# A decoder layer in split float32: Strassen's seven products for gate and up, plain products for down, the embedding projection first, SBUF placed by hand

## The chip, the cores and the metric

One core of a Trainium2 chip runs the whole program. The metric is the device time of one execution in microseconds (us); the kernel before takes 2062.82 us (median of 3 runs, 2061.0 to 2064.16). The engines are TensorE (PE, matrix products; its weight loads are PEld), VectorE (DVE), ScalarE (ACT), GpSimd (POOL) and SyncE (SP, which here only issues transfers).

## The reference

One layer over 1056 tokens (1024 of a prompt, 8 samples of 4), width 1024:

```
x = x + 1/2 * SwiGLU_1(RMSNorm(x))        # gate, up: 1024 -> 2816; down: 2816 -> 1024
z = RMSNorm(x) @ w_in                     # q, k, v | gate B | gate C | h
x = x + concat([window_attention(q, k, v), B * dwconv3(C * h)]) @ w_out
x = x + 1/2 * SwiGLU_2(RMSNorm(x))
x = x + sigmoid(RMSNorm(x) @ w_ple_gate) * (p @ w_ple_proj)      # p: 1056 x 256
```

It also returns the last keys, values and convolution inputs. All is float32; SwiGLU is (silu(h Wg) * (h Wu)) Wd.

## The kernel before

Activations lie transposed: 128 of the features in the partitions, 8 such tiles, the tokens along the row. The tokens are cut into three chunks `c` of 384, 384 and 288. Every float32 operand is kept as a high part in the fast format float32r and a low part with what is left over, and each product of two tiles takes three matmuls into one PSUM bank: high by high, high by low, low by high (`mm_group`, L264 to L270; in the convolution part `proj2`, L790 to L792). A product over 1024 inputs is thus a group of 24 matmuls.

Weights come in units of 128 x 1024 from DRAM by SP into two raw buffers, in the order in which they are used; ACT copies the high part (L110), DVE subtracts for the low part (L111), up to five units ahead. `tick` after each group splits a unit and runs deferred pieces.

The program runs: FFN 1; the input projection with attention and convolution; the output projection; FFN 2; the gated embedding. An FFN (`ffn`, L282) goes through its 22 blocks of 128 hidden features in six batches; for each block the gate and up groups of the three chunks, then DVE (L305, L307, L308), ACT (L306 tanh, L311) and POOL (L309) make the hidden tile h as a high and a low part in SBUF, then the batch's share of down is added into x by DVE (L325). The norm's factor is applied to what comes out of the products, so the products wait only for x times a gain (`prep`, L235, L236).

Attention is a list of 9 pieces of work (the samples, then 8 query blocks), which are dealt out between the halves of the convolution's groups: scores (L627, L630), scores with bias on DVE (L637), softmax on DVE, ACT and POOL (L644 to L657), transposes (L665), the product with the values (L674). One buffer each for the scores and their transposes serves all blocks. A chunk's part of the result (`mix`) is split for the output projection when its blocks are done (`split_mix`, L805, L806), and x is then read back from DRAM into a buffer of its own per chunk (L811). The output projection's groups (L878 on) add into x (L881); the first two chunks' come ahead of the third's.

The embedding projection (6 matmuls a group, L937 on) is done at the end, between the groups of the last gate. The order of each engine's instructions is set by the framework's scheduler, which simulates the program and takes from the emitted order what is ready; an engine then runs its list strictly in that order.

## Time and profile before

| | |
|---|---|
| runs | 2061.0 to 2064.16 us, median 2062.82 |
| profiled execution: span from first to last instruction | 2060.6 us (the median of the runs is 2.2 us above it; no other time of this execution is given) |
| PE busy | 2050.2 us, 12683 matmuls recorded |
| DVE, ACT, POOL busy | 960.3, 501.5, 287.2 us |
| share of PE in the chain that ended last | 97% |
| transferred | 118.06 MB, mean 57 GB/s |

The busy time of PE is the union of its matmuls' durations. These overlap: a matmul starts while the one before it still drains. What a matmul costs is therefore read from the distance between starts in the timeline and not from its mean duration. The chain of waits follows the last instruction back to what released it; its shares tell which engine's work would have to shrink.

### The profile page before, as it was taken

To read this page: it belongs to the slowest core of one execution; us is meant where nothing else is said; L and a number is where in the kernel's file an instruction comes from. 1 tells how busy PE (TensorE), PEld (TensorE's weight loads), DVE (VectorE), ACT (ScalarE), POOL (GpSimd) and SP (SyncE) were. 2 spreads that over 40 slices of the span, in tenths; PEclk is the share of its full clock that TensorE was granted. 3 is DMA by queue.
4 is the path that set the end of the run, shared out by engine and by line. 5 is a ranking of instruction groups with operands and counts; after the bars stand their busy time and mean duration, and the time that the engine had idled before them with its cause. 6 is when DMAs were issued, how large, how long until landed. Compare 5 with 4: busy or idle time off the path is not lost.

```text
span 2060.6 us, 29941 instructions
## 1 busy us (share of the span) xinstructions
PE 2050.2 (99%) x12683; PEld 2007.9 (97%) x12683; DVE 960.3 (47%) x1809; ACT 501.5 (24%) x917; POOL 287.2 (14%) x335
## 2 busy tenths in 40 slices
PE   9999999999999999999999999999999999999999
PEld 9999999999999999988888999999999999999999
DVE  6343433433334366466773764343333343344843
ACT  6121120211211243233442421212112022023410
POOL 3201010110100142022221220101101001012300
PEclk9999999999999999999999999999999999999999
DMA  7211110211111124111131211111111021111121
GB/s 263 76 54 42 52 52 11 83 41 51 43 32 62 42 102 136 35 31 32 31 93 36 70 52 41 49 38 50 40 52 52 21 72 42 31 62 52 59 71 39
DMA packets 37673, 118.06 MB, mean 57 GB/s; under 512 B 7697, under 2 KB 12185, under 8 KB 36644
## 3 DMA queue, kind: packets, MB, share of 16 engines
q1 hardware_dynamic: 35780, 112.05, 16.9%
q0 software_dynamic: 1472, 4.00, 0.7%
q8 instruction: 99, 1.62, 0.3%
q14 instruction: 34, 0.28, 0.0%
q10 hardware_dynamic: 288, 0.10, 0.0%
HBM read 106.26 MB, written 11.58 MB: 57 GB/s over the span
## 4 chain that ended last, share of the span: by engine, by line
PE 97%; DVE 2%; DMA 1%; ACT 0%; issue 0%; POOL 0%; ACTq 0%; DVEq 0%; POOLq 0%
PE ps L269 29%; PE ps L268 29%; PE ps L270 28%; PE ps L790 2%; PE ps L791 2%; PE ps L792 2%; PE ps L630 1%; PE ps L674 1%; PE ps L627 1%; PE ps L665 1%; PE ps L570 0%; DVE xnl L236 0%; DVE xr L325 0%; DVE wlo L111 0%; DVE nt L209 0%; DMA wraw<-in_wpg_dram 0%
## 5 line engine op out<-in xcount | busy, mean ns | idle before, releaser
L268 PE MATMUL ps<-xnh,whi 128*128 128x384 f32 (+1 forms) x2448 | 786.8, 322 | 1.2 <-ACT whi L110 1.2
L269 PE MATMUL ps<-xnh,wlo 128*128 128x384 f32 (+1 forms) x2448 | 786.7, 322 | 0.8 <-DVE wlo L111 0.8
L270 PE MATMUL ps<-xnl,whi 128*128 128x384 f32 (+1 forms) x2448 | 786.2, 321 | 0.0
L269 PEld LDWEIGHTS ps<-xnh,wlo 128*128 128x128 f32 x2448 | 460.0, 188 | 1.3 <-DVE wlo L111 1.1
L268 PEld LDWEIGHTS ps<-xnh,whi 128*128 128x128 f32 x2448 | 459.8, 188 | 1.5 <-ACT whi L110 1.4
L270 PEld LDWEIGHTS ps<-xnl,whi 128*128 128x128 f32 x2448 | 460.1, 188 | 0.2
L269 PE MATMUL ps<-hh,wlo 128*128 128x384 f32 (+1 forms) x1056 | 343.8, 326 | 0.0
L268 PE MATMUL ps<-hh,whi 128*128 128x384 f32 (+1 forms) x1056 | 341.5, 324 | 0.0
L270 PE MATMUL ps<-hl,whi 128*128 128x384 f32 (+1 forms) x1056 | 336.7, 320 | 0.0
L110 ACT CAST whi<-wraw 128x1024 fp32r<-128x1024 f32 x166 | 173.1, 1051 | 615.9 <-PE ps L270 523.0
L309 POOL TENSOR_TENSOR a<-a,rb 128x384 f32<-128x384 f32 x132 | 128.9, 977 | 1235.8 <-DVE a L308 1230.3
L111 DVE TENSOR_TENSOR wlo<-wraw,whi 128x1024 fp32r<-128x1024 f32 x166 | 213.5, 1290 | 106.8 <-ACT whi L110 106.6
L270 PEld LDWEIGHTS ps<-hl,whi 128*128 128x128 f32 x1056 | 198.1, 188 | 0.9 <-DVE hl L312 0.6
L269 PEld LDWEIGHTS ps<-hh,wlo 128*128 128x128 f32 x1056 | 198.1, 188 | 0.5
L268 PEld LDWEIGHTS ps<-hh,whi 128*128 128x128 f32 x1056 | 197.6, 187 | 0.3
L311 ACT CAST hh<-a 128x384 fp32r<-128x384 f32 x132 | 64.3, 487 | 366.9 <-POOL a L309 366.9
L305 DVE TENSOR_TENSOR a<-ps,rb 128x384 f32<-128x384 f32 x132 | 69.1, 524 | 178.3 <-PE ps L270 174.7
L312 DVE TENSOR_TENSOR hl<-a,hh 128x384 fp32r<-128x384 f32 x132 | 68.8, 521 | 152.0 <-ACT hh L311 152.0
L325 DVE SCALAR_TENSOR_TENSOR xr<-ps,xr 128x384 f32<-128x384 f32 (+1 forms) x144 | 75.2, 523 | 132.8 <-PE ps L270 132.6
L325 DVE SCALAR_TENSOR_TENSOR x<-ps,x 128x384 f32<-128x384 f32 (+1 forms) x144 | 75.1, 522 | 133.0 <-PE ps L270 132.9
L308 DVE TENSOR_TENSOR a<-a,ps 128x384 f32<-128x384 f32 x132 | 68.8, 521 | 126.3 <-PE ps L270 125.7
L306 ACT ACTIVATE th<-a 128x384 f32<-128x384 f32 x132 | 65.5, 496 | 225.8 <-DVE a L305 225.7
(190 smaller groups left out, 1828.6 us busy)
## 6 DMA issues: line engine op xcount, KB each, us to landing
wraw<-in_w1gu_dram SPq DMA_DIRECT2D x44, 512.0 KB
wraw<-in_w2gu_dram SPq DMA_DIRECT2D x44, 512.0 KB
wraw<-in_w1d_dram SPq DMA_DIRECT2D x22, 512.0 KB
wraw<-in_w2d_dram SPq DMA_DIRECT2D x22, 512.0 KB
wraw<-in_win_dram SPq DMA_DIRECT2D x18, 512.0 KB
xtok<-in_xtok_dram SPq DMA_DIRECT2D x8, 512.0 KB
wraw<-in_wout_dram SPq DMA_DIRECT2D x8, 512.0 KB
wraw<-in_wpg_dram SPq DMA_DIRECT2D x8, 512.0 KB
```

The source lines that it names most:

```text
L110: nc.scalar.copy(out=hi, in_=raw)
L111: nc.vector.tensor_tensor(out=lo, in0=raw, in1=hi.bitcast(F32), op=ALU.subtract)
L268: nc.tensor.matmul(ps[:, :W], lhsT=wh, rhs=xh, start=(k == 0), stop=False)
L269: nc.tensor.matmul(ps[:, :W], lhsT=wl, rhs=xh, start=False, stop=False)
L270: nc.tensor.matmul(ps[:, :W], lhsT=wh, rhs=xl, start=False, stop=(k == n - 1))
L305: nc.vector.tensor_tensor(out=a[:, :W], in0=psg[:, :W], in1=rb, op=ALU.mult)
L306: nc.scalar.activation(out=th[:, :W], in_=a[:, :W], func=AF.Tanh, scale=0.5)
L308: nc.vector.tensor_tensor(out=a[:, :W], in0=a[:, :W], in1=ps[:, :W], op=ALU.mult)
L309: nc.gpsimd.tensor_tensor(out=a[:, :W], in0=a[:, :W], in1=rb, op=ALU.mult)
L311: nc.scalar.copy(out=hh[j][:, sl], in_=a[:, :W])
L312: nc.vector.tensor_tensor(out=hl[j][:, sl], in0=a[:, :W], in1=hh[j][:, sl].bitcast(F32), op=ALU.subtract)
L325: nc.vector.scalar_tensor_tensor(out=x[c][:, m], in0=ps[:, :W], scalar=0.25, in1=x[c][:, m], op0=ALU.mult, op1=ALU.add)
```

## The change

**Gate and up.** The first three blocks of hidden features are still computed plainly (`lead_group`), now as 2 x 2 quarters: two output rows (gate, up), two halves of the inputs, two halves of a token chunk. Tokens are cut into two chunks of 528 here, with halves of 264. For the other 19 blocks Strassen's scheme (in Winograd's form) replaces the 8 quarter products by 7 (`Quad`, `segment`): each is 4 tiles x 3 matmuls of 264 columns. The four weight sums are made by POOL per block, the four sums of activations once per chunk; all are split into high and low parts as before. A segment interleaves products 1, 5, 2, 6 of one chunk with 7, 3, 4 of the one before.

**Down.** h goes to DRAM (`hd`) and comes back in chunks of 384, 384 and 288; down runs over two halves of 11 hidden tiles, in groups of 33 matmuls (`DownProj`).

**Norms of the FFNs.** Their factor is now multiplied into x in place before the products (`n_stat`, `n_y`); x is read again from DRAM for down.

**Embedding projection.** It runs first, as 32 half groups of 6 matmuls, and its result waits in DRAM (`pp_d`).

**Memory.** `at` places nearly everything by hand in one arena. In the output projection x is one region again, over the place of `mix`; its units 22 to 25 (rows m = 4 to 7) have their weights where the keys, the values and the bias lay (`WOUT2`). The order is chunk by chunk.

The core of the diff:

```diff
+    def unit_at(i):
+        return WOUT2[i - 22] if 22 <= i < 26 else UAT[(i - 26 if i > 25 else i) % 4]
     def can_split():
-        return st["split"] < len(units) and st["split"] < st["done"] + HL
+        i = st["split"]
+        room = st["done"] >= 18 if 22 <= i < 26 else i < st["done"] + HL
+        return i < st["end"] and room
...
+    OPS = (1, 5, 2, 6, 7, 3, 4)
+    class Weights:
+        def __init__(self, gu, j):
+            r = wload(gu, j)
+            s = [at("ws", WS + 512 * i, 512) for i in range(4)]
+            add = nc.gpsimd.tensor_tensor
+            add(out=s[0], in0=r[2], in1=r[3], op=ALU.add)
+            add(out=s[1], in0=s[0], in1=r[0], op=ALU.add)
+            add(out=s[2], in0=r[0], in1=r[2], op=ALU.add)
+            add(out=s[3], in0=s[1], in1=r[1], op=ALU.add)
+            self.of = {1: r[0], 2: r[1], 3: s[3], 4: r[3], 5: s[0], 6: s[1], 7: s[2]}
+            self.w = {}
+        def split(self, o):
+            self.w[o] = whl(WAT[o])
+            split(self.w[o][0], self.w[o][1], self.of[o])
+        def __getitem__(self, o):
+            return self.w[o]
...
+    class Quad:
+        def __init__(self, w, c):
+            self.w, self.ch, self.follow = w, c, None
+        def product(self, o, ps, start):
+            wh, wl = self.w[o]
+            for k in range(4):
+                ks = slice(k * P, (k + 1) * P)
+                last = k == 3
+                bh, bl = op_k(self.ch, o, 0, k), op_k(self.ch, o, 1, k)
+                nc.tensor.matmul(ps[:, :HH], lhsT=wh[:, ks], rhs=bh, start=(start and k == 0), stop=False, skip_group_check=True)
+                nc.tensor.matmul(ps[:, :HH], lhsT=wl[:, ks], rhs=bh, start=False, stop=False, skip_group_check=True)
+                nc.tensor.matmul(ps[:, :HH], lhsT=wh[:, ks], rhs=bl, start=False, stop=last, skip_group_check=True)
+        def step(self, o):
+            if o == 1:
+                self.b = psb()
+            elif o == 5:
+                self.c = psb()
+            elif o == 2:
+                self.a = psb()
+            ps = self.b if o in (1, 6, 7, 4) else self.c if o in (5, 3) else self.a
+            self.product(o, ps, o in (1, 5, 2))
+            getattr(self, f"out{o}")()
+            if self.follow:
+                self.follow.split(o)
+    def segment(q, p):
+        for o, of in ((1, q), (5, q), (7, p), (2, q), (6, q), (3, p), (4, p)):
+            if of:
+                of.step(o)
...
+    class GateUp(Quad):
+        def __init__(self, w, j, c):
+            super().__init__(w, c)
+            self.j = j
+            self.g = g_tile()
+        def silu(self, i):
+            th = th_tile()
+            g = self.g[:, i]
+            nc.scalar.activation(out=th, in_=g, func=AF.Tanh, scale=0.5)
+            nc.vector.scalar_tensor_tensor(out=g, in0=th, scalar=1.0, in1=g, op0=ALU.add, op1=ALU.mult)
+        def out1(self):
+            nc.scalar.copy(out=self.g[:, 0], in_=self.b[:, :HH])
+        def out5(self):
+            pass
+        def out2(self):
+            nc.vector.tensor_tensor(out=self.g[:, 0], in0=self.a[:, :HH], in1=self.g[:, 0], op=ALU.add)
+            self.silu(0)
+        def out6(self):
+            nc.scalar.copy(out=self.g[:, 1], in_=self.b[:, :HH])
+        def out7(self):
+            self.u = wtile("u", shape=[P, HH])
+            nc.vector.tensor_copy(out=self.u, in_=self.c[:, :HH])
+            nc.vector.scalar_tensor_tensor(out=self.u, in0=self.b[:, :HH], scalar=-1.0, in1=self.u, op0=ALU.mult, op1=ALU.subtract)
+        def out3(self):
+            nc.vector.tensor_tensor(out=self.g[:, 1], in0=self.c[:, :HH], in1=self.g[:, 1], op=ALU.add)
+            self.silu(1)
+            nc.gpsimd.tensor_tensor(out=self.g[:, 1], in0=self.g[:, 1], in1=self.u, op=ALU.mult)
+        def out4(self):
+            nc.vector.scalar_tensor_tensor(out=self.g[:, 0], in0=self.b[:, :HH], scalar=-1.0, in1=self.g[:, 0], op0=ALU.mult, op1=ALU.mult)
+            nc.sync.dma_start(out=hd[self.j, :, self.ch * HC:(self.ch + 1) * HC], in_=self.g.rearrange("p i t -> p (i t)"))
...
+    def n_y(c, kp, g, j):
+        for i in range(2):
+            kk = 2 * kp + i + 4 * j
+            nc.vector.scalar_tensor_tensor(
+                out=chunk(kk, c), in0=chunk(kk, c), scalar=vec[:, g + kk:g + kk + 1], in1=nrb[c], op0=ALU.mult, op1=ALU.mult,
+            )
+        for h in range(2):
+            split_op(c, ((1, 0), (2, 3))[j][h], kp, block(c, 2 * kp + 4 * j, h))
+    def n_t5(c, kp):
+        t = tmp3("nt1")
+        nc.gpsimd.tensor_tensor(out=t, in0=block(c, 2 * kp, 0), in1=block(c, 2 * kp, 1), op=ALU.subtract)
+        split_op(c, 5, kp, t)
...
+    def gate_up(gu, g, lw, steps, before_end):
+        lead = {0: lw}
+        bg = list(steps)
+        def run(j, c, per=1):
+            for _ in lead_group(lead[j], j, c, g_tile()):
+                for _ in range(per):
+                    if bg:
+                        bg.pop(0)()
+                now[0] += 1
+        n1 = len(bg)
+        lead[1] = lead_weights(gu, 1)
+        run(0, 0, -(-n1 // 8))
+        run(1, 0, -(-n1 // 8))
+        while bg:
+            bg.pop(0)()
+        for kp in range(2):
+            for f in (n_t5, n_t7, n_t6, n_t4):
+                bg.append(lambda f=f, kp=kp: f(0, kp))
+        for kp in range(2):
+            bg.append(lambda kp=kp: n_t5(1, kp))
+        run(0, 1)
+        lead[2] = lead_weights(gu, 2)
+        run(1, 1)
+        run(2, 0)
+        while bg:
+            bg.pop(0)()
+        run(2, 1)
+        w = Weights(gu, LEAD)
+        for o in OPS:
+            w.split(o)
+        for kp in range(2):
+            for f in (n_t7, n_t6, n_t4):
+                f(1, kp)
+        prev = None
+        for j in range(LEAD, FF):
+            for c in range(2):
+                q = GateUp(w, j, c)
+                if c and j + 1 < FF:
+                    q.follow = w = Weights(gu, j + 1)
+                segment(q, prev)
+                prev = q
+                before_end(j, c)
+        segment(None, prev)
...
+    drain()
+    for k in range(KT):
+        nc.sync.dma_start(out=X[k], in_=xm_d[:, k])
...
-    for c in (0, 1):
-        for m in range(5):
+    for c in range(3):
+        for m in range(KT):
             out_group(m, c)
...
```

On three places the two kernels' lists are set side by side. In names, the number behind `a` is the place in the arena, `bh` and `bl` are high and low parts of an operand of a Strassen product, `wh` and `wl` those of a weight.

PE, inside FFN 1, before: the end of one down group and the start of the next (`hh`, `hl` are the hidden tile's parts).

```order
L270 MATMUL ps_2904<-hl_2694,whi_2704 128x384
L268 MATMUL ps_2918<-hh_2114,whi_2421 128x384
L269 MATMUL ps_2918<-hh_2114,wlo_2422 128x384
L270 MATMUL ps_2918<-hl_2115,whi_2421 128x384
L268 MATMUL ps_2918<-hh_2311,whi_2513 128x384
L269 MATMUL ps_2918<-hh_2311,wlo_2514 128x384
```

PE, inside FFN 1, now: in the gate and up part, product 1 of one chunk, two matmuls of product 7 of the chunk before, product 5.

```order
L413 MATMUL ps_1633<-bh1_0_a8976_476,wl_a38400_316 128x264
L414 MATMUL ps_1633<-bl1_0_a10032_477,wh_a37888_315 128x264
L412 MATMUL ps_1524<-bh7_1_a35776_1426,wh_a34752_565 128x264
L413 MATMUL ps_1524<-bh7_1_a35776_1426,wl_a35264_566 128x264
L412 MATMUL ps_1647<-bh5_0_a14784_927,wh_a31680_323 128x264
L413 MATMUL ps_1647<-bh5_0_a14784_927,wl_a32192_324 128x264
```

The matmuls of gate and up are 264 columns wide where before all had 384 or 288.

DVE at the start of FFN 1, before: the low parts of x (`xnl`), weights (`wlo`), then the first gate (L305).

```order
L236 SCALAR_TENSOR_TENSOR xnl_156<-x_108,vec,xnh_155 128x384 x2
L111 TENSOR_TENSOR wlo<-wraw,whi 128x1024 x2
L236 SCALAR_TENSOR_TENSOR xnl_156<-x_108,vec,xnh_155 128x384 x6
L414 TENSOR_SCALAR tst<-tst 128x3
L236 SCALAR_TENSOR_TENSOR xnl_228<-x_131,vec,xnh_227 128x384 x8
L305 TENSOR_TENSOR a<-ps,rb 128x384
```

DVE at the start of FFN 1, now: x scaled (L572), sums of squares of the second chunk (L535), lead weights (L381), operands of the first chunk (L335), and the last copies of the embedding's results (L816).

```order
L572 SCALAR_TENSOR_TENSOR x_a_72<-x_a_72,vec,rb 128x528 x8
L381 TENSOR_TENSOR wl_a_562<-wr_a_555,wh_a_561 128x512
L535 TENSOR_TENSOR acc<-acc,sq 128x528
L816 COPY po_a_115<-ps 128x264
L381 TENSOR_TENSOR wl_a_566<-wr_a_557,wh_a_565 128x512
L381 TENSOR_TENSOR wl_a_570<-wr_a_307,wh_a_569 128x512
L335 TENSOR_TENSOR bl_0_a_450<-x_a_72,bh_0_a_449 128x528
L816 COPY po_a_116<-ps 128x264
L335 TENSOR_TENSOR bl_0_a_454<-x_a_72,bh_0_a_453 128x528
```

The embedding's copies out of PSUM now stand behind the scaling of x, which itself stands behind the norm's sums; PE's embedding groups and its first lead group need both.

PE at the start of the output projection, before: the last block's transposes and values, between output groups of the second chunk (`mh`, `ml`).

```order
L269 MATMUL ps<-mh_9507,wlo 128x384
L665 MATMUL ps<-ident,S 128x128 x4
L674 MATMUL ps<-PT,vtm 64x512
L270 MATMUL ps<-ml_9508,whi 128x384
L268 MATMUL ps<-mh_9507,whi 128x384
L269 MATMUL ps<-mh_9507,wlo 128x384
L270 MATMUL ps<-ml_9508,whi 128x384
L268 MATMUL ps<-mh_9507,whi 128x384
L269 MATMUL ps<-mh_9507,wlo 128x384
L674 MATMUL ps<-PT,vtm 64x512 x2
```

PE at the same place, now: the values of block 6 end, one matmul of the fifth output group, the transposes and values of block 7, then the fifth group goes on (`whi_a_10914`, `wlo_a_10915` are its weights).

```order
L1100 MATMUL ps<-PT_a_9253,vtm_a_7956 64x512
L306 MATMUL ps<-xnh_a_6944,whi_a_10914 128x384
L1091 MATMUL ps<-ident,S_a_9150 128x128 x8
L1091 MATMUL ps<-ident,S_a_9153 128x128 x8
L1100 MATMUL ps<-PT_a_9233,vtm_a_7956 64x512
L1100 MATMUL ps<-PT_a_9253,vtm_a_7956 64x512
L1100 MATMUL ps<-PT_a_9233,vtm_a_7956 64x512
L1100 MATMUL ps<-PT_a_9253,vtm_a_7956 64x512
L307 MATMUL ps<-xnh_a_6944,wlo_a_10915 128x384
```

Only four output groups and one matmul of a fifth stand between the last convolution group and the last block's values; before, output groups ran alongside all of it. From block 6's transposes on, nothing but that one matmul stands between the attention pieces.

## Rows read from the trace of the kernel before

**Rows 1.** The page, head and busy time of the engines
```profile
span 2060.6 us, 29941 instructions
...
PE 2050.2 (99%) x12683; PEld 2007.9 (97%) x12683; DVE 960.3 (47%) x1809; ACT 501.5 (24%) x917; POOL 287.2 (14%) x335
```

**Rows 2.** Grouped lines of PE, shapes apart: busy us, mean ns of one
```profile
L268 PE MATMUL ps<-xnh,whi 128*128 128x384 f32 x1632 | 546.7, 335 | 1.2 <-ACT whi L110 1.2
```

**Rows 3.** Windows: length, busy us and count per engine, granted clock, DMA share, GB/s
```profile
8.00:12.00 4.00, 3.18 (x13) 3.01 (x13) 4.00 (x6) 4.00 (x8) 0.00 (x0) 0.76 1.03 409
12.00:20.00 8.00, 8.00 (x43) 8.00 (x43) 5.05 (x11) 7.19 (x15) 3.79 (x11) 0.91 1.02 413
...
1940.00:1960.00 20.00, 17.19 (x92) 15.48 (x91) 18.50 (x42) 6.58 (x9) 2.59 (x2) 1.00 0.57 178
```

**Rows 4.** Timeline of PE, FFN 1: start us, length us, instruction
```profile
299.75 0.29 PE L268 MATMUL ps<-xnh,whi 128*128 128x288 f32 x1
...
302.15 0.34 PE L268 MATMUL ps<-xnh,whi 128*128 128x384 f32 x1
...
303.89 0.33 PE L269 MATMUL ps<-xnh,wlo 128*128 128x384 f32 x1
```

**Rows 5.** Timeline of PE, transposes in the attention part
```profile
999.97 1.03 PE L665 MATMUL ps<-ident,S 128*128 128x128 f32 x8
1000.76 0.38 PE L790 MATMUL ps<-xnh,whi 128*128 128x288 f32 x1
```

**Rows 6.** Chain of waits: start us, length us, piece
```profile
822.13 0.81 PE ps L517 x12
822.94 0.69 PE ps L506 x6
...
1096.18 1.87 PE ps L674 x8
...
1117.90 1.00 PE ps L674 x2
...
1158.48 0.65 PE ps L248 x2
```

**Rows 7.** Grouped lines of DVE, shapes apart
```profile
L111 DVE TENSOR_TENSOR wlo<-wraw,whi 128x1024 fp32r<-128x1024 f32 x166 | 213.5, 1290 | 106.8 <-ACT whi L110 106.6
...
L305 DVE TENSOR_TENSOR a<-ps,rb 128x384 f32<-128x384 f32 x88 | 49.0, 557 | 128.1 <-PE ps L270 124.7 <-ACT rb L429 3.3
```

**Rows 8.** Timeline of PE, first product
```profile
7.73 0.44 PE L268 MATMUL ps<-xnh,whi 128*128 128x384 f32 x1 [1.15 <-ACT whi L110]
```

**Rows 9.** Grouped lines of POOL, shapes apart
```profile
L309 POOL TENSOR_TENSOR a<-a,rb 128x384 f32<-128x384 f32 x88 | 91.3, 1038 | 1137.4 <-DVE a L308 1131.9 <-ACT th L306 5.5
```

**Rows 10.** Line L792: shortest/median/longest ns, first to last start
```profile
L792 PE MATMUL ps<-xnl,whi x288: 290/334/447, 860.6 to 1057.4; 128*128 128x384 f32 x96, 128*128 128x288 f32 x48
```

**Rows 11.** Timeline of PE, scores of one block
```profile
1058.15 0.28 PE L627 MATMUL ps<-ks,qh 128*128 128x256 f32 x1
...
1059.30 0.44 PE L268 MATMUL ps<-mh,whi 128*128 128x384 f32 x1
```

**Rows 12.** Timeline of DVE, softmax of the last block
```profile
1096.28 2.33 DVE L644 TENSOR_REDUCE mx<-S 128x4 f32<-128x1024 f32 x2
```

**Rows 13.** Timeline of POOL, softmax of the last block
```profile
1102.35 1.89 POOL L657 TENSOR_TENSOR S<-S,den 128x1024 f32<-128x1024 f32 x1 [10.75 <-DVE den L656]
1104.64 1.89 POOL L657 TENSOR_TENSOR S<-S,den 128x1024 f32<-128x1024 f32 x1 [0.40 <-DVE den L656]
```

**Rows 14.** Grouped lines of ACT, shapes apart
```profile
L110 ACT CAST whi<-wraw 128x1024 fp32r<-128x1024 f32 x166 | 173.1, 1051 | 615.9 <-PE ps L270 523.0 <-DMA wraw<-in_w2gu_dram 28.0 <-DMA wraw<-in_w1gu_dram 25.4
...
L311 ACT CAST hh<-a 128x384 fp32r<-128x384 f32 x88 | 45.2, 514 | 346.2 <-POOL a L309 346.2
```

**Rows 15.** Line L806, the same view as in rows 10
```profile
L806 DVE TENSOR_TENSOR ml<-mix,mh x24: 446/546/2244, 1025.7 to 1121.7; 128x384 fp32r<-128x384 f32 x16, 128x288 fp32r<-128x288 f32 x8
```

**Rows 16.** Line L309, the same view as in rows 10
```profile
L309 POOL TENSOR_TENSOR a<-a,rb x132: 798/1012/2707, 28.7 to 1889.3; 128x384 f32<-128x384 f32 x88, 128x288 f32<-128x288 f32 x44
```

More of the change, by code (lines that the diff above doesn't have):

```diff
@@ new lines, in lead_weights, with op_at @@
+    def lead_weights(gu, j):
+        r = wload(gu, j)
+        places = [WAT[6], WAT[7], WAT[3], WS] if j % 2 else [WAT[1], WAT[2], WAT[5], WAT[4]]
+        w = []
+        for i in range(4):
+            w.append(whl(places[i]))
+            nc.scalar.copy(out=w[i][0], in_=r[i])
+            nc.vector.tensor_tensor(out=w[i][1], in0=r[i], in1=w[i][0].bitcast(F32), op=ALU.subtract)
+        return w
+    def op_at(c, o):
+        if c == 1 and o in (5, 6):
+            k0 = 4 * (o - 5)
+            return [[(k0 + 2 * part + kp) * NT for kp in range(2)] for part in range(2)]
+        return [[OPAT[c][o] + 1056 * part + 528 * kp for kp in range(2)] for part in range(2)]
@@ new lines, in tile_decoder_layer @@
+    wsrc = lambda k: wpp[k]
+    psrc = lambda k: pv[:, k]
+    s0, s1 = slice(0, 512), slice(512, 1024)
+    t0_, t1_ = slice(0, HC), slice(HC, NT)
+    pe_load(qraw, wsrc, s0)
+    pe_load(praw, psrc, t0_)
+    pe_split(qraw, qh, ql, s0)
+    pe_split(praw, ph, pl, t0_)
+    pe_load(praw, psrc, t1_)
+    pe_load(qraw, wsrc, s1)
+    for k in range(KT):
+        nc.sync.dma_start(out=chunk(k, 0), in_=xin[:, k, 0:HC])
+    for m in range(4):
+        pe_group(m, 0)
+    pe_split(praw, ph, pl, t1_)
@@ new lines, in tile_decoder_layer, with chunk1_steps @@
+    for m in range(4):
+        pe_group(m, 1)
+    pe_split(qraw, qh, ql, s1)
+    for k in range(KT):
+        n_square(0, k)
+    lw1 = lead_weights(w1gu, 0)
+    for k in range(KT):
+        nc.sync.dma_start(out=chunk(k, 1), in_=xin[:, k, HC:NT])
+    steps0 = chunk0_steps(G1)
+    for m in range(4, 8):
+        for c in range(2):
+            pe_group(m, c)
+            if m > 4 and steps0:
+                steps0.pop(0)()
+    while steps0:
+        steps0.pop(0)()
+    def chunk1_steps(g, squares):
+        s = [lambda k=k: n_square(1, k) for k in range(KT)] if squares else []
+        s.append(lambda: n_stat(1))
+        return s + [lambda kp=kp, j=j: n_y(1, kp, g, j) for j in range(2) for kp in range(2)]
@@ new lines, in mid_hook @@
+    def mid_hook(m, c):
+        square(c, m)
+        if c == 0:
+            prep(0, m, GM)
+        if c == 2:
+            nc.sync.dma_start(out=xm_d[:, m], in_=X[m])
+        if m == 6 and c == 2:
+            st["end"] = 2
+        if m == KT - 1:
+            norm_r(c, "nm", 9, 4 if c < 2 else 2)
+            if c:
+                prep(c, m, GM)
+            if c < 2:
+                for k in range(KT - 1):
+                    prep(c + 1, k, GM)
+    dp = DownProj(w1d, xin, mid_hook)
@@ L459, in tile_decoder_layer, with at_end @@
+    def at_end(j, c):
+        if j == 8 and c == 1:
+            bias_table()
+        dp.early(j, c)
+    gate_up(w1gu, G1, lw1, chunk1_steps(G1, True), at_end)
+    dp.run()
+    st["end"] = 26
+    mix = [at("mix", KT * CS[c], KT * CW[c]).rearrange("p (k w) -> p k w", k=KT) for c in range(3)]
     U0 = UNIT["win"]
     ks = [slot(0, [P, 1056], F32R, "ks0"), slot(10, [P, 1056], F32R, "ks1")]
-    kend = const.tile([P, 160], F32, name="kend")
+    kend = at("kend", 31520, 160)
     vtm = slot(1, [P, 8, P], F32, "vtm")
-    vsm = const.tile([NS, P], F32, name="vsm")
+    vsm = at("vsm", 45056, P, rows=NS)
@@ L928, in tile_decoder_layer, with ple_hook @@
-    after(2, pe_split)
+            tick()
+            if c == 1:
+                n_square(0, m)
+                nc.sync.dma_start(out=xs_d[:, m, 0:HC], in_=X[m][:, 0:HC])
+            if c == 2:
+                n_square(1, m)
+                nc.sync.dma_start(out=xs_d[:, m, HC:NT], in_=X[m][:, HC:NT])
+                if steps0:
+                    steps0.pop(0)()
+                if m == 4:
+                    lw2 = lead_weights(w2gu, 0)
+    drain()
+    def ple_hook(m, c):
+        square(c, m)
+        if c == 0:
+            prep(0, m, GP)
+        if m == 6 and c == 2:
+            st["end"] = 28
+        if m == KT - 1:
+            norm_r(c, "np", 9, 4 if c < 2 else 2)
+            if c:
+                prep(c, m, GP)
+            if c < 2:
+                for k in range(KT - 1):
+                    prep(c + 1, k, GP)
```

632 lines of the change are left out of this document (362 added, 270 removed).

## The prediction

> **What bounds the kernel now.** I read the page's head first: PE is busy for 2050.2 of 2060.6 us, DVE for 47% of the span, ACT for 24%, POOL for 14% [rows 1]. So the end is set by how many matmuls PE issues and how far apart, and other engines matter where PE waits for them. The grouped lines cannot price a matmul: 384 columns show a mean of 335 ns [rows 2], but 1632 of those alone would be 546.7 us, and they overlap. Next the windows: the clock is 0.76 and 0.91 of its upper level (2.4 GHz) in the first two and 1.00 late in the run, even where PE is busy for only 17.19 of 20 us [rows 3]. Then PE's timeline, for the distance between starts: 18 matmuls of 288 columns take 302.15 - 299.75 = 2.40 us, 133.3 ns each, and 10 of 384 take 1.74 us; with 173.4 for those a column costs 0.417 ns, one cycle at 2.4 GHz, and a matmul has 13.3 ns besides [rows 4]. A weight load is not what spaces them: 8 transposes of 128 columns, each with its own, take 0.79 us, 98.75 ns each [rows 5].
>
> **Gate and up.** Before, each FFN has 22 blocks x 2 x 3 chunks x 24 = 3168 matmuls: 2112 x 0.1734 + 1056 x 0.1333 = 507.0 us. Now 576 in the lead blocks and 19 x 2 x 7 x 12 = 3192 in Strassen's, 3768 of 264 columns. At 264 x 0.4167 + 13.3 = 123.3 ns that is 464.7 us; 42.3 less, **-84.6** for two. No row has 264 columns. Bounds: 133.3 ns as for 288 (507.0 - 502.3 saves 4.7 per FFN, 9.4 in all) and 122.2 ns, in proportion to 288 (93 in all). I take the line through both widths.
>
> The Trainium skill, "TensorE: Matmul & The Clock Gate", section "Back-to-back issue gap", gives N/2.4 + 2.5 ns for a warm clock. Here the remainder is 13.3 ns [rows 4], so the trace does not agree; by the page's figure gate and up would save 97.4 us, and the sum would be about 13 us lower. The measurement decides.
>
> **Down** keeps its products, in other groups: 0. **Embedding**: 192 x 0.1233 = 23.7 for 96 x 0.1734 + 48 x 0.1333 = 23.0: **+0.7**.
>
> **Norms.** The nearest small matmuls take 0.81 / 12 = 0.068 us (broadcast of a factor) and 0.69 / 6 = 0.115 us (column sums) [rows 6]. Each FFN chunk now has 12 column sums and 6 broadcasts, 1.79 us, four times 7.1. Three products of 0.65 [rows 6] and three broadcasts as long go, 3.9: **+3.2**.
>
> **Front of FFN 1.** DVE prices: 128x1024 costs 1290 ns, 128x384 from PSUM 557 [rows 7], so by the line through both about 0.42 us for 264, 0.70 for 512 and 0.72 for 528. Ahead of the first lead group DVE has 8 splits of the embedding's operands (5.7), 16 copies (6.7), 6 additions of squares (4.3), 8 lead weights (5.6), 8 scalings of x (5.8), 8 operand splits (5.8) and 12 small ones (1.8): 35.7 us. From 7.7, where the first product starts [rows 8], that ends at 43.4; PE's embedding ends at 7.7 + 23.7 = 31.4. The difference, 12, and a weight split behind it make **+13**. Bounds 4 (half of the additions and copies fall beside waits that were there anyway) and 20 (the loads: 409 GB/s are moved here already [rows 3]).
>
> **The second chunk's operands** are made beside the first lead groups, each of 12 x 8 matmuls, 11.8 us; DVE has some 8 scalings and 8 splits, 11.6, beside lead weights, 5.6, and POOL's sums, at 1038 ns for 384 columns [rows 9], so about 2.8 for 1056. I put 5 in FFN 1 and 2 in FFN 2: **+7** (0 to 12).
>
> **h through DRAM.** Stores and reloads take the queues of SP beside PE, and 413 GB/s is shown [rows 3], so a hidden tile of 270 KB is 0.65 us in flight. Only at the four changes from gate/up to down, or half to half, does the last block's chain (product 4, DVE, store, reload, split) stand in the way: **+4** for four (0 to 12). The restored x and the stores of sums are covered by PE; cost 0.
>
> **Output projection.** Before, the convolution's last group starts at 1057.4 [rows 10] and the last values end at 1118.9 [rows 6]: 61 us with output groups in between. Now only four groups, 4 x 24 x 0.1734 = 16.6 us, and one matmul can run there (the order above): the fifth unit's weights lie where the keys and the bias were, and x comes back over `mix` after its last split. A block's pieces: scores 16 x 0.29 = 4.6 [rows 11]; softmax 10.25, from 1096.28 [rows 12] to 1104.64 + 1.89 [rows 13]; 16 transposes 1.6 [rows 5]; copies about 0.7; values 1.87 [rows 6]. About three blocks are left after the convolution, and as one buffer of scores serves all, I take them in a row behind one block's scores: 4.6 + 3 x 10.25 + 3 x 4.2 = 48, and 2 for hand-overs, 50 us. PE has 16.6 + 2 x 8.1 for the scores, transposes and values of two blocks + 3 of leftovers = 36: a wait of 14. Behind it the fifth unit's low part costs DVE 1.3 [rows 7] after ACT's 1.05 [rows 14]; and the last splits of `mix`, five at 0.55 [rows 15], and 540 KB of x, 1.3 at 413 GB/s, 4 in all, delay the first sums, on which PE waits when its PSUM buffers are full. Sum **+20**. Bounds 8 (the blocks overlap as before; only weights and x show) and 31 (two blocks without cover, 36, less the hidden half of the weights' part).
>
> **Clock.** The front, where the rows show 0.76 for 4 us and 0.91 for 8, costs 4 x 0.24 + 8 x 0.09 = 1.7 us [rows 3]. Three new waits of that sort: **+5** (2 to 8).
>
> **The seam from FFN 2 to the gate, and the other norms**: what was waited for there is waited for again; 0 (-3 to 6, by the one factor broadcast and its chain).
>
> **Strassen's segments.** There are 76, of 84 x 0.1233 = 10.36 us. For each block of two, 20.7 us, DVE has 14 ops on 264 columns at 0.42 and 7 weight splits at 0.70: 10.8; ACT 7.6, 7 x 0.62 + 8 x 0.41 by 0.514 for 384 and 1.051 for 1024 [rows 14]; POOL 4 weight sums and 2 products, 4 x 1.38 + 2 x 0.71 = 6.9 [rows 9]. None is full, and a PSUM buffer is wanted again two products, 2.96 us, after its end. I put **+4** for single misses (0 to 15).
>
> Sum: -84.6 + 0.7 + 3.2 + 13 + 7 + 4 + 20 + 5 + 0 + 4 = -27.7. On 2060.6 that is 2032.9; the median of the runs is 2.2 above the span: **2035**.
>
> **Rivals.**
> The first: the waits are mostly hidden. At their lower ends (front 4, second chunk 0, switches 0, output 8, clock 2, seams 0, segments 0) they are 14 and not 53: 1996, and near 2000. For it: DVE is 47% busy, and the scheduler works in what is ready. Against it: in the output projection the order leaves nothing to put in.
>
> The second: they stand at their upper ends (front 18, second chunk 10, switches 8, output 29, clock 7, seams 2, segments 8: 82 and not 53), 2064, no change. For it: each estimate of a wait counts one chain, and two that meet at one place add.
>
> The third ends slower. A segment's weights come through POOL's sums, ACT's copy and DVE's difference, and the outputs through DVE and POOL in turn. POOL's product with 384 columns takes 798 ns alone but up to 2707 [rows 16], and DVE's difference with two operands in SBUF 446 and up to 2244 [rows 15]: they stretch where they meet. If they exclude each other, a segment has 5.4 of DVE and 3.5 of POOL in one line, 8.9, and with about 2.1 us of waits for ACT's parts between them more than the 10.36 that PE needs. From (2062.8 - 2035) / 76 = 0.37 us of wait per segment the change is a loss; at 0.65 each it is 49 more: 2084. Against it: most of DVE's ops there read PSUM, and the median stays near the shortest.
>
> The Trainium skill, "SBUF — State Buffer", section "Who interferes with whom", says that DVE and GpSimd share a pair of ports under an exclusive lock. By that rule the third rival holds; the stretched rows [rows 15, 16] agree with it, their medians show how seldom it strikes in this kernel.
>
> The fourth: 264 columns are no cheaper than 288. Then the first term is -9.4: 2035 + 75 = 2110.
>
> **Numbers.** Forecast 0.60; waits hidden 0.20; upper ends 0.08; POOL against DVE 0.09; width 0.03. The forecast's own range is 2018 to 2052. For 8 in 10 I take 1998 to 2068: it leaves out a third of the first rival (0.06), the far side of the second (0.02), most of the third (0.08) and the fourth, 0.19 together. What a measurement of this kernel can tell from no change is about 0.2%, 2058.7 to 2067. Faster: 0.60 + 0.20 + the near side of the second, 0.02 = 0.82. Same: its middle, 0.04, and the near end of the third, 0.01. Slower: 0.02 + 0.08 + 0.03 = 0.13.
>
> **What would show it.** In the profile after: starts of 264-column matmuls 123 ns apart (133 speaks for the fourth rival); a segment of 10.4 to 10.5 us, and PE's waits inside it on DVE's outputs or low parts (over 0.37 us per segment, the third); idle time of PE of about 12 us between the embedding and the first lead group, with DVE busy throughout; two or three gaps together near 14 us ahead of the last values, and one of about 4 for x after the fifth output group; no idle time at h's reloads beyond 1 us each. PE's busy time should fall by about 80. I am wrong if the gaps of the output projection stay under 5 or exceed 35, or if the segments wait regularly.

## The result

The changed kernel takes 2034.53 us (median of 4 runs, 2031.85 to 2038.38) against 2063.4 us before: a ratio of 0.9861, 95% interval 0.9847 to 0.9875, 1.4% faster. 2035 was forecast. The profiled execution, the shortest of the four, spans 2029.9 us, 30.7 less than [rows 1]. Two executions further down, one of x1_rotate (2758.11 us) and that of x6_noembed (2145.35 us), had a lower granted clock throughout (0.65 and 0.84 in the mean), and their times are left out.

Head and busy time of the engines after:

```profile
span 2029.9 us, 34765 instructions
...
PE 1986.7 (98%) x14051; PEld 1939.6 (96%) x14051; DVE 1066.5 (53%) x2057; ACT 653.2 (32%) x1334; POOL 479.3 (24%) x414
```

PE's busy time fell by 63.5 us, the span by half of that: PE idled 10 us before and idles 43 now. By stage, from the starts of PE's matmuls on the timelines of both:

| stage | before | after | difference |
|---|---|---|---|
| FFN 1 (after: with the embedding projection) | 776.7 | 775.0 | -1.8 |
| input projection, to the first convolution group | 83.4 | 88.7 | +5.3 |
| convolution, attention, output projection | 311.7 | 343.3 | +31.6 |
| FFN 2 | 764.3 | 717.1 | -47.2 |
| gate (before: with the embedding projection) | 124.4 | 105.8 | -18.6 |

FFN 2 shows the change at its best, the third row what it costs. First the timeline of PE in a segment (start, length, instruction), the rows that answer to [rows 4]:

```profile
300.24 0.28 PE L412 MATMUL ps<-bh_a,wh_a 128*128 128x264 f32 x1
...
310.47 0.29 PE L412 MATMUL ps<-bh_a,wh_a 128*128 128x264 f32 x1
```

84 matmuls lie between these starts, 10.23 us: 121.8 ns each, and 121.7 over the longer stretch of x5_plain below; 121.7 is used from here on. Windows over both runs of segments and over the last attention blocks (columns as in [rows 3]):

```profile
132.00:520.00 388.00, 388.00 (x3183) 387.22 (x3182) 219.89 (x407) 141.23 (x298) 133.64 (x118) 1.00 0.29 91
1282.00:1668.00 386.00, 386.00 (x3172) 386.00 (x3171) 216.14 (x401) 139.20 (x293) 127.57 (x107) 1.00 0.28 86
...
1084.00:1104.00 20.00, 15.58 (x45) 8.96 (x43) 8.21 (x21) 6.50 (x21) 3.79 (x2) 0.60 0.00 0
1104.00:1129.00 25.00, 13.01 (x53) 9.13 (x52) 10.36 (x23) 10.84 (x29) 3.79 (x2) 0.77 0.35 120
```

In the segments PE is never idle, at a clock of 1.00. From 1084 to 1129 it is busy for 28.6 of 45 us, at 0.60 and 0.77. The same matmuls take longer there. Two scores (L1053, L1056) and the values of one block (L1100) ahead of the first of these windows, and the values of the next block in it:

```profile
1070.88 0.38 PE L1053 MATMUL ps<-ks_a,qh_a 128*128 128x256 f32 x1
1071.19 0.38 PE L1056 MATMUL ps<-ks_a,ql_a 64*128 64x256 f32 x1
...
1078.29 1.94 PE L1100 MATMUL ps<-PT_a,vtm_a 128*64 128x512 f32 x8
...
1100.92 3.68 PE L1100 MATMUL ps<-PT_a,vtm_a 128*64 128x512 f32 x8
```

What PE waits for, from the list of its waits (engine, line, released by: us in total, times, longest):

```profile
PE ps L1091 <- POOL S_a L1083: 9.3, 4, 4.6
PE ps L306 <- issue: 5.7, 1, 5.7
PE ps L306 <- DVE pth L1366: 4.5, 2, 4.1
PE ps L810 <- ACT po_a L814: 3.7, 3, 2.2
PE ps L501 <- DVE bl_a L335: 3.3, 3, 2.1
PE ps L944 <- DVE kms L931: 2.7, 1, 2.7
...
PE ps L810 <- DVE po_a L816: 2.3, 2, 2.0
PE ps L307 <- DVE wlo_a L161: 1.4, 1, 1.4
```

The first two are the last attention blocks and the wait behind them, the third the gate, the sixth the input projection, the last the low part of the fifth output unit, the others the front. No line of the segments (L412 to L414) is in the list. DVE behind the last values: the last splits of `mix`, then the first two sums of the fifth output row, which wait for x:

```profile
1119.39 1.56 DVE L1231 TENSOR_TENSOR xnl_a<-mix_a,xnh_a 128x288 fp32r<-128x288 f32 x4
...
1127.28 0.56 DVE L1307 TENSOR_TENSOR x_a<-x_a,ps 128x384 f32<-128x384 f32 x1 [0.81 <-DMA x_a<-xm_d]
1128.52 0.56 DVE L1307 TENSOR_TENSOR x_a<-x_a,ps 128x384 f32<-128x384 f32 x1 [0.68 <-DMA x_a<-xm_d]
```

In the chain of waits, a score in the slow stretch, and the norms' small products between the output projection and FFN 2 (start, length, piece):

```profile
1096.40 0.51 PE ps L1056
...
1213.00 1.89 PE ps L548 x22
...
1220.45 1.73 PE ps L558 x12
```

### The profile page after: what moved, and what is told of

Its sections match the earlier page's. It is cut to its first block, busy times and chain, and to the rows that moved or that the text cites. A ratio compares the mean times of both kernels' runs of the same rounds, so it can differ in the third digit from the quotient of the medians.

```text
span 2029.9 us, 34765 instructions
## 1 busy us (share of the span) xinstructions
PE 1986.7 (98%) x14051; PEld 1939.6 (96%) x14051; DVE 1066.5 (53%) x2057; ACT 653.2 (32%) x1334; POOL 479.3 (24%) x414
## 4 chain that ended last, share of the span: by engine, by line
PE 93%; DVE 5%; ACT 1%; issue 1%; DMA 1%; POOL 0%; SPq 0%; ACTq 0%; POOLq 0%; DVEq 0%
PE ps L412 13%; PE ps L413 13%; PE ps L414 13%; PE ps L306 12%; PE ps L307 12%; PE ps L308 12%; PE ps L1217 2%; PE ps L1218 2%; PE ps L1216 2%; PE ps L501 2%; PE ps L499 2%; PE ps L500 2%; PE ps L1056 1%; DVE bl_a L335 1%; PE ps L1053 1%; PE ps L1100 1%
## 5 line engine op out<-in xcount | busy, mean ns | idle before, releaser
L413 PE MATMUL ps<-bh_a,wl_a 128*128 128x264 f32 x2128 | 603.7, 284 | 0.0
L412 PE MATMUL ps<-bh_a,wh_a 128*128 128x264 f32 x2128 | 602.2, 284 | 0.0
L414 PE MATMUL ps<-bl_a,wh_a 128*128 128x264 f32 x2128 | 597.7, 284 | 0.0
L412 PEld LDWEIGHTS ps<-bh_a,wh_a 128*128 128x128 f32 x2128 | 399.9, 188 | 0.6 <-issue 0.6
L413 PEld LDWEIGHTS ps<-bh_a,wl_a 128*128 128x128 f32 x2128 | 399.8, 188 | 0.0
L414 PEld LDWEIGHTS ps<-bl_a,wh_a 128*128 128x128 f32 x2128 | 399.0, 189 | 0.0
L307 PE MATMUL ps<-hh_a,dwl_a 128*128 128x384 f32 (+1 forms) x1056 | 338.8, 321 | 0.0
L306 PE MATMUL ps<-hh_a,dwh_a 128*128 128x384 f32 (+1 forms) x1056 | 337.7, 321 | 0.0
L308 PE MATMUL ps<-hl_a,dwh_a 128*128 128x384 f32 (+1 forms) x1056 | 337.7, 321 | 0.0
L308 PEld LDWEIGHTS ps<-hl_a,dwh_a 128*128 128x128 f32 x1056 | 198.5, 188 | 0.0
L306 PE MATMUL ps<-xnh_a,whi_a 128*128 128x384 f32 (+1 forms) x528 | 175.2, 332 | 10.5 <-issue 5.7
L335 DVE TENSOR_TENSOR wl_a<-ws_a,wh_a 128x512 fp32r<-128x512 f32 x152 | 107.9, 710 | 58.9 <-ACT wh_a L334 54.2
L335 DVE TENSOR_TENSOR wl_a<-wr_a,wh_a 128x512 fp32r<-128x512 f32 x114 | 105.9, 929 | 30.0 <-ACT wh_a L334 26.3
L359 POOL TENSOR_TENSOR ws_a<-wr_a,wr_a 128x512 f32<-128x512 f32 x38 | 52.3, 1377 | 257.9 <-DMA wr_a<-in_w2gu_dram 122.2
```

What stands on the lines that cost most here:

```text
L306: nc.tensor.matmul(ps[:, :W], lhsT=wh, rhs=xh, start=(k == 0), stop=False)
L307: nc.tensor.matmul(ps[:, :W], lhsT=wl, rhs=xh, start=False, stop=False)
L308: nc.tensor.matmul(ps[:, :W], lhsT=wh, rhs=xl, start=False, stop=(k == n - 1))
L335: nc.vector.tensor_tensor(out=lo, in0=src, in1=hi.bitcast(F32), op=ALU.subtract)
L359: add(out=s[0], in0=r[2], in1=r[3], op=ALU.add)
L412: nc.tensor.matmul(ps[:, :HH], lhsT=wh[:, ks], rhs=bh, start=(start and k == 0), stop=False, skip_group_check=True)
```

## The experiments

All times are medians, to be compared with 2034.5 for the kernel changed. Stretches are read from the profiled executions.

### The last attention blocks: weights or cover

**x1_rotate.** 

> The weights of the output projection's rows m = 4 to 7 are placed anew: the first over the bias, the next over the scores and their transposes, the last over keys and values, where before the first had the keys and values. Theory (PE waits after the last values because the fifth unit cannot be split until keys and values are free, and the next raw load waits for that split): the gaps of 1.95 us at 1116.0 and 6.04 us at 1121.9 go, 4 to 9 us less, about 2028 on the scale of 2034.5. Rival (x comes back only after the last split of mix, 4.3 MB at about 410 GB/s are 10.5 us, and PE stops at five full PSUM buffers anyway): 0 to 2 us less, and the gap moves to the sixth group of the fifth row.

```diff
-WOUT2 = [21504 + 2048 * i for i in range(4)]
+WOUT2 = [23616, 25728, 27840, 21504]
```

2029.91 us, ratio to the kernel before 0.984 [0.9823, 0.9856], which overlaps that of the kernel changed. The median is 4.6 us lower, where the runs of the kernel changed lie 6.5 us apart; the span is 1.9 us shorter, and the stretch from the first convolution group to FFN 2 takes 341.9 us and not 343.3. The two gaps became one, 9.4 us from start to start, on x (waits of PE):

```profile
PE ps L306 <- DVE x_a L1307: 8.9, 1, 8.9
```

The rival holds: with the weights early, PE stops at its full PSUM buffers until x is back, which can be loaded only after the last split of `mix`. In that stretch the weights' place alone is worth 1.5 us.

**x2_early.** 

> The first four rows of the output projection are done for both of the first chunks ahead of the rest; their sums go through small buffers and DRAM, so they need neither x in its place nor the weights of rows 4 to 7. Theory (the attention pieces of blocks 6 and 7 stand alone because PE has only four groups to put between them): the second four groups, 16.6 us, move into the stretch 1084 to 1122, the two waits for the softmax (4.4 and 5.3 us) shrink to under 2 together, the clock there stays at 1.00, and the time falls by 8 to 20 us, about 2020. Rival (the chain of block 6 and 7 through scores, softmax, transposes and values sets the end of this part, and PE's groups were only behind it): the last values end no earlier and the time stays within 3 us of 2034.5.

```diff
+    def out_early(m, c):
...
+        t = wtile("xo")[:, :W]
+        nc.sync.dma_start(out=t, in_=xm_d[:, m, cols(c)])
+        ps = proj(UO + m, c)
+        nc.vector.tensor_tensor(out=t, in0=t, in1=ps[:, :W], op=ALU.add)
+        nc.sync.dma_start(out=xm_d[:, m, cols(c)], in_=t)
...
+    for c in (0, 1):
+        for m in range(4):
+            out_early(m, c)
+            tick()
```

2012.54 us, ratio 0.9759 [0.9743, 0.9776]: 22 us less, 2 beyond the theory's range. The same two windows:

```profile
1084.00:1104.00 20.00, 20.00 (x113) 18.05 (x111) 6.15 (x15) 4.64 (x16) 3.79 (x2) 1.00 0.11 40
1104.00:1129.00 25.00, 17.97 (x82) 12.76 (x82) 11.93 (x25) 10.96 (x30) 3.79 (x2) 0.86 0.23 67
```

PE now has work, at full clock, through the first, and the last matmul of the values starts at 1120.3 (1116.0 in the kernel changed), later and not earlier; yet FFN 2 starts 21.9 us sooner, since 16.6 us of output groups are done by then. (2.0 of the 21.9 were gained ahead of the convolution, where the two kernels are alike.) So it was cover that was missing; the wait for x is covered too and is no longer in PE's list. One wait is left, 5.35 us for block 7's softmax at 1113.9, where the theory had under 2.

### The segments

**x5_plain.** 

> All 22 blocks of gate and up are done as the lead blocks are, with 8 quarter products and no weight sums; everything else stays (the first down weights come one group later). Theory (what the segments save is the number of matmuls and nothing is given back in them): 19 x 2 x 12 x 2 = 912 more matmuls at 0.1218 us, 111 us more, plus 2 to 5 at the two starts of down: about 2148, some 85 above the kernel before. Rival (DVE, ACT and POOL in the segments cost part of the gain, hidden in the spacing of the matmuls): less than 95 us more, under 2130, and a spacing of plain 264-column matmuls below that of the segments' 0.1218.

```diff
-        w = Weights(gu, LEAD)
...
+        for j in range(3, FF):
+            lead[j] = lead_weights(gu, j)
             for c in range(2):
...
-                segment(q, prev)
...
+                run(j, c)
```

2151.92 us, 4.3% above the kernel before (ratio 1.0428). 121.5 us more span: 912 x 0.1217 = 111.0, 6 at the starts of down and 2 before the lead, with some 2 not traced. The spacing of the plain matmuls is the segments' own (384 between 300.20 and 346.92: 121.7 ns), so the theory holds: what DVE, ACT and POOL do in a segment costs PE nothing. It also shows that everything else in the change, without Strassen's products, is a loss of some 88 us.

**x7_pool2.** 

> In each of Strassen's blocks POOL does four more additions of 512 columns and a fill on a tile that nobody else reads, some 6 us more per block of 20.5 us, on top of the four weight sums. Theory (POOL and DVE stretch each other now and then, but the segments have slack and PE sees nothing of it): POOL's busy time rises by about 220 us, the time stays within 3 us of 2034.5, and the waits of PE in the segments stay under 3 us in all. Rival (DVE and POOL exclude each other there: 10.8 us of DVE and 12.9 of POOL in one line are 23.7 us for a block in which PE needs 20.5): about 3 us more per block, some 110 more, 2140.

```diff
+            self.jk = wtile("jk", shape=[P, 512])
+            nc.gpsimd.memset(self.jk, 0.0)
...
+            if o in (5, 2, 6, 4):
+                nc.gpsimd.tensor_tensor(out=self.jk, in0=self.jk, in1=self.jk, op=ALU.add)
```

2033.01 us: no difference, with POOL busy for 679.9 us and not 479.3. DVE is stretched all the same, but not all of it. Grouped lines of DVE in the kernel changed (busy us, mean ns):

```profile
L460 DVE SCALAR_TENSOR_TENSOR g_a<-th_a,g_a 128x264 f32<-128x264 f32 x152 | 73.7, 485 | 38.5 <-ACT th_a L459 38.5
...
L469 DVE TENSOR_TENSOR g_a<-ps,g_a 128x264 f32<-128x264 f32 x76 | 32.8, 432 | 41.0 <-PE ps L414 38.7
```

The same two in x7_pool2:

```profile
L464 DVE SCALAR_TENSOR_TENSOR g_a<-th_a,g_a 128x264 f32<-128x264 f32 x152 | 99.4, 654 | 38.5 <-ACT th_a L463 38.5
...
L473 DVE TENSOR_TENSOR g_a<-ps,g_a 128x264 f32<-128x264 f32 x76 | 32.9, 432 | 31.5 <-PE ps L418 29.3
```

With both inputs in SBUF the mean goes from 485 to 654 ns; with one in PSUM it stays at 432. DVE's busy time rises by 44 us (1066.5 to 1110.3), all hidden: from 130 to 520 us DVE is busy for 241.1, POOL for 222.3 and PE for 390.0 of 390 us. DVE and POOL together are more than the stretch, so they did not exclude each other.

### The front

**x3_front.** 

> At the front the norm of the first chunk (squares, sums, factor) and the scaling and splitting of its operands are emitted ahead of the second part of the embedding groups, which fill in. Theory (the first lead group waits for a chain, sums to factor to broadcast to scaling to low parts, that is held up at each step by embedding copies, squares of the second chunk and weight parts that stand ahead of it in the lists): the first lead group starts at 38 to 44 us and not at 50.5, 4 to 12 us less, about 2027. Rival (DVE's work in the front as a whole, some 36 us, sets it, whatever its order): the embedding's last groups or the second lead block wait in its place, 0 to 2 us less.

```diff
+    steps0 = chunk0_steps(G1)
+    for k in range(KT):
+        n_square(0, k)
+    steps0.pop(0)()
     for m in range(4):
         pe_group(m, 0)
```

2035.15 us: nothing. It decides little, since the scheduler left the order nearly as it was; the lead starts at 51.3.

**y4_front8.** 

> As x3_front (norm of the first chunk emitted first), with eight buffers in place of four for the embedding's results. Theory (copies out of PSUM, and with them PE's embedding groups and the broadcast behind them, wait for stores that stand behind 14 MB of loads in one queue): the waits of PE on L814 and L816, 6 us together, go; the broadcast comes 3 to 5 us earlier, the lead starts at 44 to 47 and the time falls by 3 to 6 us, about 2030. Rival (DVE's 17 us from the first scaling to the last low part and the copies set the start): the lead still starts at 49 to 51, within 2 us of 2034.5.

```diff
-pout = [at("po", PL + 12480 + 528 * i, 528) for i in range(4)]
+pout = [at("po", PL + 12480 + 528 * i, 528) for i in range(8)]
-        o = pout[pn[0] % 4]
+        o = pout[pn[0] % 8]
```

2034.36 us: again nothing, but now by another way. The embedding ends at 38.6 and not at 50.4, the lead starts at 41.8 and not at 50.5: theory right so far. But its second group (96 matmuls each) starts at 63.2, as in the kernel changed, and the third at 80.4 (77.9), as PE waits for DVE's parts one after the other. Windows of the kernel changed:

```profile
0.00:20.00 20.00, 16.99 (x115) 16.10 (x115) 12.93 (x24) 13.94 (x25) 5.58 (x8) 0.99 0.93 330
20.00:40.00 20.00, 15.50 (x98) 14.66 (x98) 11.61 (x27) 10.56 (x23) 4.30 (x3) 0.84 0.71 266
40.00:60.00 20.00, 17.36 (x123) 16.75 (x124) 16.61 (x26) 6.02 (x15) 6.91 (x3) 0.83 0.39 135
60.00:100.00 40.00, 36.10 (x266) 34.93 (x265) 30.80 (x53) 14.42 (x28) 13.21 (x8) 0.91 0.08 26
```

The second and third in y4_front8:

```profile
20.00:40.00 20.00, 18.90 (x145) 18.32 (x143) 11.61 (x29) 10.38 (x25) 4.19 (x4) 0.91 0.90 340
40.00:60.00 20.00, 13.71 (x72) 12.50 (x73) 16.21 (x23) 6.64 (x14) 6.91 (x4) 0.66 0.21 66
```

PE is busier before 40 and idles after it, while DVE is busy for 16.21 of 20 us. The rival is wrong on the start and right on the time: DVE's operands decide, not the embedding's buffers.

**x6_noembed.** 

> Leaves out the embedding projection: its loads, splits, 192 matmuls, copies and stores; the gate's result is multiplied by x in its place. Theory (the first lead group waits for a chain through loads, norm and DVE, in which copies, loads and stores of the embedding stand at several places): the first lead group starts at 28 to 35 and not at 50.5, 15 to 22 us less. Rival 1 (PE's work is what the front costs): the start moves by the 23.4 us of the 192 matmuls or more, to 27 or below. Rival 2 (the norm's own chain sets the start and the embedding only fills it): it moves by less than 10.

```diff
-    pe_load(qraw, wsrc, s0)
...
-    for m in range(4, 8):
-        for c in range(2):
-            pe_group(m, c)
...
-        nc.sync.dma_start(out=pproj[m], in_=pp_d[:, m])
+        nc.sync.dma_start(out=pproj[m], in_=xin[:, m])
```

The lead starts at 29.3, 21.2 earlier, as the theory has it. The total is taken from the repetition, x6b_noembed.

**x6b_noembed.** 

> x6_noembed once more, since TensorE ran the whole of that one execution at a granted clock of 0.84, so that only its first 30 us could be read. Leaves out the embedding projection; the gate's result is multiplied by x in its place. Theory (the embedding takes 23.4 us of PE and its copies, stores and splits stand in the chain to the operands, but behind the lead group PE is then held by operands that DVE makes one by one): the lead starts 20 to 22 us earlier than at 50.5, and 5 to 10 of that are given back by the third lead group: 2019 to 2025. Rival (nothing given back): 2011 to 2015.

2017.25 us, 17.3 less, between the theory's range and the rival's, 2 from each. The lead starts at 29.6, 20.9 earlier, and FFN 1's down at 505.1, 15.4 earlier. So the embedding's 23.4 us of matmuls cost about 16 there, the rest fills waits. PE's waits of x6b_noembed:

```profile
PE ps L499 <- ACT bh_a L334: 7.8, 1, 7.8
PE ps L548 <- POOL acc L535: 5.8, 1, 5.8
PE ps L501 <- DVE bl_a L335: 4.9, 2, 2.9
```

These are the norm's chain with nothing beside it.

### The norms behind down

**x4_stat.** 

> The sums of squares ahead of the input projection and of the last gate are issued one group after their chunk is done, and no longer four. Theory (since down runs row by row over all chunks, the three norms come due together at its end, and the late sums put two of the three factor chains on DVE at once, 795 to 808): the 3.0 us wait at 804.8 and part of the 4.4 us wait at 1949.4 go, 3 to 7 us less, about 2030. Rival (DVE is full there in any order, with operand low parts and weight low parts): within 2 us of 2034.5.

```diff
-            norm_r(c, "nm", 9, 4 if c < 2 else 2)
+            norm_r(c, "nm", 9, 1)
...
-            norm_r(c, "np", 9, 4 if c < 2 else 2)
+            norm_r(c, "np", 9, 1)
```

2024.43 us, ratio 0.981 [0.9796, 0.9825], 10.1 less where the theory had 3 to 7. The span is 5.0 us shorter; the execution profiled here is the longest of its four, that of the kernel changed the shortest of its four. At the gate the wait of 4.1 us is gone; the window there in the kernel changed:

```profile
1943.00:1957.00 14.00, 9.53 (x56) 9.07 (x55) 13.21 (x37) 3.60 (x6) 0.00 (x0) 0.81 0.32 99
```

And in x4_stat, at the same distance from the end of down:

```profile
1946.00:1960.00 14.00, 14.00 (x93) 14.00 (x92) 11.68 (x26) 4.37 (x7) 0.00 (x0) 1.00 0.63 198
```

From the last down group to the last matmul it is 93.4 us and not 101.2. At the input projection the 2.7 us wait turned into one of 1.3 for the values; its stretch takes 86.7 us and not 88.7, but the next one 1.6 more, and FFN 2 starts no earlier (1207.3 and 1207.0): the theory holds for the gate alone.

### Put together

**y5_best.** 

> Put together: weights of rows 4 to 7 placed as in x1_rotate, eight early output groups as in x2_early, early sums as in x4_stat, front as in y4_front8, and two lead blocks in place of three. If the gains add (22 of x2_early, 4 of the last wait for block 7 that a full group now covers, 8 of x4_stat at the gate, 5.8 for 48 matmuls in 2 FFNs fewer, 3 at the front): about 1994. If operands of the second chunk are late with one lead block less, 3 to 6 us of it go: 2000.

1999.25 us, the second of the two figures. One lead block less (`LEAD = 2`) is given back: PE waits 3.8 us at 107.5 and 1.8 in FFN 2 for the first weights of the segments.

**y6_best3.** 

> As y5_best, with three lead blocks as in the kernel changed. Theory (one lead block less saved 48 matmuls in each FFN, 5.8 us, but PE then waited 5.6 us for the first weights of the segments): within 3 us of y5_best's 1999. Rival (the third block costs its matmuls): 2003 to 2006.

1997.01 us, with three lead blocks, the same within the measurement.

**z4_chunk1.** 

> As y6_best3; and the squares and the norm of the second chunk are emitted in the first half of the first lead group, and all copies of the embedding's results go to ACT, half of which DVE did. Theory (beside the first lead groups PE waits for operands that DVE makes one after the other, and DVE had 8 copies, 3.4 us, and a stop of 3 us for the second chunk's factor ahead of them): 3 to 7 us less than y6_best3. Rival (the second chunk's work now stands ahead of the first's low parts and only changes places with them): within 2 us of y6_best3.

```diff
-            if h:
-                nc.scalar.copy(out=o[:, h * HH:(h + 1) * HH], in_=ps[:, :HH])
-            else:
-                nc.vector.tensor_copy(out=o[:, h * HH:(h + 1) * HH], in_=ps[:, :HH])
+            nc.scalar.copy(out=o[:, h * HH:(h + 1) * HH], in_=ps[:, :HH])
...
-        run(0, 0, -(-n1 // 8))
-        run(1, 0, -(-n1 // 8))
+        run(0, 0, 5)
+        run(1, 0, 2)
```

1991.03 us (1986.66 to 1993.11), ratio to the kernel before 0.9642 [0.9629, 0.9655], 6 less than y6_best3: the theory. The fourth lead group starts at 85.3 (93.3 in y6_best3). The run makes two changes at once, and which of them gave the 6 us is not shown. Of this kernel, the head, and the wait for the softmax in the list of PE's waits:

```profile
span 1984.9 us, 34781 instructions
...
PE 1966.4 (99%) x14051; PEld 1922.7 (97%) x14051; DVE 1054.7 (53%) x2041; ACT 656.9 (33%) x1350; POOL 478.9 (24%) x414
```

```profile
PE ps L1087 <- POOL S_a L1079: 2.4, 2, 1.2
```

It is the fastest version that was run: 43.5 us below the kernel changed. It issues the same 14051 matmuls, but PE is busy for 1966.4 us and not 1986.7.

## Why the prediction was right

The time came out to half a microsecond, which is more than the reasons deserve: the mechanism held, several terms did not, and their errors cancelled. The runs of the kernel changed alone lie 6.5 us apart. Waits here are a stage's time less its matmuls, at the spacing of the upper clock level (2.4 GHz); so they hold what a lower clock costs too, and the shares of the clock and the small terms of the forecast are put to their stages.

| term | predicted | measured |
|---|---|---|
| gate and up, matmuls | -84.6 | -96.9 (7536 x 0.1217 = 917.1 for 1014.0) |
| embedding, matmuls | +0.7 | +0.4 |
| norms of the FFNs | +3.2 | +10.5 (4 x 3.6, less the 3.9 as forecast) |
| waits of FFN 1 (front 13, second chunk 5, others) | +23.7 | +18 |
| waits of FFN 2 | +6 | -1.1 |
| input projection | 0 | +5.3 |
| attention and output projection, with its clock | +23.3 | +28.7 |
| gate, without the embedding | 0 | +4.4 |
| sum | -27.7 | -30.7 (span: -30.7) |

**Gate and up.** Right in kind: the gain is the number of matmuls times their spacing, which x5_plain shows from the other side. The size was off by 12 us: 264 columns take 121.7 ns, not 123.3, just under the lower bound (122.2, in proportion to 288). Beyond the column time of 110.0 that leaves 11.7 ns, still far from the 2.5 that the Trainium skill ("TensorE: Matmul & The Clock Gate", "Back-to-back issue gap") adds in its formula for an isolated matmul at a warm clock. Why 264 has less besides than 288 is open.

**Segments and changes to down.** The +4 and +4 were nothing: PE waits nowhere in 388 and 386 us of segments, nor in the two downs (busy for all 255 us from 520 to 775 and all 256 from 1668 to 1924). The third rival falls with x7_pool2. The shortest times that I gave for it, 798 and 446 ns, are not those of 384 columns but of the 288 in the same rows; 384 take at least 1007 and 542. The Trainium skill's rule ("SBUF — State Buffer", "Who interferes with whom") names the right operations, those of DVE with both inputs in SBUF (485 to 654 ns; 432 unchanged with one in PSUM), and they have the slack to be stretched. The rival's fault was to add DVE and POOL up as if all of DVE were excluded.

**Norms.** Mis-sized: a product of plain float32 operands is two instructions in the trace. The 12 column sums of a chunk are 24 records, 22 of them in 1.89 us, and the 6 broadcasts 12 in 1.73; I had counted products and priced them by records of [rows 6], which are halves.

**Clock.** Mis-sized, and it made up for the waits. By number and spacing the matmuls are 86.0 us less work (-96.9 + 0.4 + 10.5), but PE's busy time fell by 63.5, and not by the 80 that I had named as a sign. That leaves some 22 us (an estimate from these numbers) of matmuls that took longer, as the values above did, 3.68 us and not 1.94, where the granted clock was down to 0.60; z4_chunk1, with few waits, gets 20.3 back for the same number of matmuls. I had put 5 for the clock, 8 at most. PE's idle time rose by 32.8 us, where my terms without the clock add up to 48. In the output projection it is 16.4 us of waits (9.3, 5.7 and 1.4) for my 20, and about 12 for the clock for my 3.3.

**Front.** The wait was there, a little smaller, but not as told, and not all of it was waiting: up to 132 us PE idles for 14.0 us (3.1 before), so 7 of the 18 go with the clock (0.84 and 0.83 from 20 to 60). The lead follows 0.1 us behind the embedding, with no idle time between. DVE was not busy throughout: 24.5 of the first 40 us. The embedding's groups ran until 50.4 instead of 31.4, held by their result buffers, and the norm's chain ran beside them. y4_front8 takes that hold away and gains nothing, since the operands' low parts come next; z4_chunk1 relieves DVE and starts the second chunk's norm sooner, and gains 6. So DVE's work does set this stretch, but spread over the first 100 us (busy for 16.6 of 20 from 40 on and for 30.8 of 40 from 60 on), not as 35.7 us in one piece before the lead.

**Output projection.** Right in place, cause and about in size: two waits for a softmax (4.1 and 4.6 us), a clock down to 0.60, and one gap of 5.7 us behind the values. x2_early shows the cause, the missing cover; x1_rotate that the weights' place, to which I gave 2.4 us, hides the wait for x. (The fifth unit's weights lie where the keys and the values were; I had written the bias.) That wait I sized with 1.3 us for one of eight tiles of x. The tiles do come about 1.3 us apart, but the first sum waits until 1127.3 for the first of them, the last split being over at 1121.0: 6.3 us. What holds the first tile is not shown.

**What I missed.** The input projection (+5.3) and the gate (+4.4). Down's second half now goes row by row over all three chunks, where before it went chunk by chunk, so that the three norms come due together; I wrote "what was waited for there is waited for again". x4_stat gets the gate's part back. At the gate the embedding's groups had also been the filler, by the order of the lists; no run puts them back there.
